# Two attention and MLP blocks on one core: the instruction order from the framework's timeline-simulating scheduler

## The chip, the cores and the metric

The kernel runs on one core of a Trainium2 chip. The metric is the device time of one execution in microseconds (us), the median of several runs. A core has five engines that run side by side: PE multiplies matrices (its weight loads are shown as PEld), DVE and ACT work elementwise, POOL does small set-up work, and SP here only issues DMAs. Each engine works off its own list of instructions strictly in the order of the list; semaphores make it wait for the others.

## The reference

Two models of depth 2 are run one after the other on one sequence of 256 tokens, width 1,024, in float32: first a block of attention layers (no MLP), then a block of attention and MLP layers.

```python
def first_block(x, ...):          # DEPTH = 2
    x = even_layer(x, ...)        # differential attention (4 heads) + forgetting attention (8)
    x = odd_layer(x, ...)         # sliding window with sinks (8) + chunked, relative bias (8)
def second_block(x, ...):         # DEPTH = 2
    x = x + dsa_mixer(rms_norm_2(x, g0), ...)          # index scores, top 64 keys, 16 heads
    x = x + squared_relu_mlp(rms_norm_2(x, m0), ...)   # 1024 -> 4096 -> 1024
    x = x + mla_mixer(rms_norm_2(x, g1), ...)          # latent q and kv, 16 heads
    x = x + squared_relu_mlp(rms_norm_2(x, m1), ...)
    return rms_norm_2(x, final_norm)
```

Every layer is: norm, projection in, attention per head (scores, bias or mask, softmax, weighted sum), projection out, residual. An MLP is `relu(h @ w_up)` squared, times `w_down`.

## The kernel before

**Work.** The state x lies transposed in SBUF (`xT`, 128 partitions x 8 x 256). Every product runs in a three-part form on rounded operands: each float32 operand is split into a rounded high part and a low rest, and PE adds high x high, low x high and high x low. So each weight block of 128 x 1,024 is fetched by a DMA on SP (`fetch`, L127, tile `raw`, 4 buffers), copied to its high part by ACT (`wh`, L176, 4 buffers), and its rest is taken by DVE (`wl`, L177, 4 buffers), in pieces of 256 or 512 columns (`PIECE`). PE then multiplies in `tokens` (L200), `tokens_apart` (L217) or `features` (L231); the sums stand in PSUM banks: `mm` 3, `s` 2, `tp` 2, `pv` 1 (`PS_BUFS`).

**Stages.** `forward` sets the layer number N.layer to 0 to 5: even layer, odd layer, sparse attention, MLP, latent attention, MLP. The stages lie at about 0 to 180, 180 to 300, 300 to 400, 400 to 580, 580 to 662 and 662 to 866 us; the projection out of one stage overlaps the next. In an attention stage a head's softmax goes: scores on PE (L506 or L518, bank `s`), adding the bias and taking the minimum of the negated scores on DVE (L534, `sx`, `mx`), exponential on ACT (L537, `se`), division (L545, L547), three transposes on PE (L553 to L555, bank `tp`), a split by ACT and DVE (L556, L557, `pt`), and the weighted sum on PE (L572, L587, L589, L606, L610, bank `pv`). Norms end in a reciprocal root, which `rsqrt` works out in nine short steps on DVE (L110 to L120); the head norm then scales `u` (L447), which PE transposes (L399).

**What sets the order.** Nothing in the code fixes the order on an engine. The functions are traced in one sequence; inside an attention stage that is a string of unit names (`ORDER0` to `ORDER3`), for example AW = weights of a head of the differential attention, BT = transposes of a forgetting head, GG = a gate. Every traced instruction gets a priority, its place in the trace; `N.ahead` moves it forward or back by an offset of the table `AHEAD` (weight splits under the key W). [...]

[...]

The change touches the function `kernel`, at the line that opens the `TileContext` (L1506).

## Time and profile before

| | |
|---|---|
| median of 3 runs | 866.77 us (865.86, 866.77, 868.64) |
| the profiled execution's own time | 868.05 us |
| its span, first to last instruction | 866.4 us |
| instructions | 17,641, of them 6,554 matmuls and as many weight loads |
| busy: PE, PEld, DVE, ACT, POOL | 97%, 93%, 77%, 67%, 5% of the span |
| DMA | 138.09 MB, 159 GB/s on average |
| granted TensorE clock, mean | 0.996 of full speed |

The profile is one execution with every instruction's start and length. A group names the line, the engine, the operation and its tiles (`out<-in`); a matmul's end is modelled and includes the time in the pipeline, so the records of neighbouring matmuls overlap. "Idle before" is the time in which the engine stood still ahead of these instructions, with the work that released it. [...]

### The profile page before, as it was taken

The numbers are of one execution on the slowest core, as the hardware profiler recorded it, in microseconds if no ns is written. First come the engines' busy times: TensorE is split into PE (matmuls) and PEld (weight loads), VectorE is DVE, ScalarE is ACT, GpSimd is POOL, SyncE is SP. The second block draws the span as 40 slices with busy tenths as digits, with TensorE's granted clock in tenths as the row PEclk, the third lists the DMA queues.
The fourth block names the chain that finished last, engine by engine and source line by source line (L and its number), as shares of the span: only waits on it lengthen the run. The fifth ranks groups of instructions, "written<-read, shape, count | busy, mean of one in ns | idle before, by whom it ended". The sixth has DMA issues, their size and how long they took to land. (4 is left out here: it accounts for less than half of the span.)

```text
span 866.4 us, 17641 instructions
## 1 busy us (share of the span) xinstructions
PE 840.8 (97%) x6554; PEld 808.7 (93%) x6554; DVE 670.6 (77%) x1799; ACT 577.7 (67%) x1379; POOL 40.7 (5%) x90
## 2 busy tenths in 40 slices
PE   6899999999999999999999999998999999999996
PEld 6899999999999999899999999998999998899986
DVE  6779997889898789988665576678999865557654
ACT  6597985779796576976654455556997665346542
POOL 9100000001000100000000000002000000000000
PEclk9999999999999999999999999999999999999999
DMA  7544344644634632246656656543324565555651
GB/s 263 166 161 139 107 142 158 198 158 143 230 97 160 184 108 91 97 137 184 191 194 190 180 192 194 187 139 104 112 73 157 183 190 180 186 187 184 218 163 48
DMA packets 40677, 138.09 MB, mean 159 GB/s; under 512 B 4960, under 2 KB 7152, under 8 KB 40592
## 3 DMA queue, kind: packets, MB, share of 16 engines
q1 hardware_dynamic: 39456, 134.20, 47.9%
q0 software_dynamic: 848, 2.25, 0.9%
q8 instruction: 51, 0.84, 0.4%
q10 hardware_dynamic: 288, 0.52, 0.2%
q14 instruction: 34, 0.28, 0.1%
HBM read 135.91 MB, written 1.05 MB: 158 GB/s over the span
## 5 line engine op out<-in xcount | busy, mean ns | idle before, releaser
L176 ACT ACTIVATE wh<-raw 128x512 fp32r<-128x512 f32 (+2 forms) x548 | 289.8, 570 | 202.8 <-issue 103.2
L177 DVE TENSOR_TENSOR wl<-raw,wh 128x512 fp32r<-128x512 f32 (+2 forms) x548 | 322.4, 618 | 115.6 <-ACT wh L176 111.9
L231 PE MATMUL mm<-ar,wh 128*128 128x256 f32 (+1 forms) x1664 | 301.0, 281 | 0.5 <-ACT ar L714 0.5
L231 PEld LDWEIGHTS mm<-ar,wh 128*128 128x128 f32 (+1 forms) x1664 | 255.0, 188 | 2.0 <-ACT ar L714 1.3
L200 PE MATMUL mm<-wh,ar 128*128 128x256 f32 (+2 forms) x1168 | 237.4, 299 | 8.1 <-ACT wh L176 6.6
L231 PE MATMUL mm<-ar,wl 128*128 128x256 f32 x832 | 232.8, 281 | 0.0
L200 PEld LDWEIGHTS mm<-wh,ar 128*128 128x128 f32 x1168 | 187.9, 192 | 13.4 <-ACT wh L176 6.7
L200 PE MATMUL mm<-wl,ar 128*128 128x256 f32 (+2 forms) x584 | 173.9, 298 | 1.1 <-DVE wl L177 1.1
L231 PEld LDWEIGHTS mm<-ar,wl 128*128 128x128 f32 x832 | 155.9, 188 | 0.3 <-DVE wl L177 0.2
L200 PEld LDWEIGHTS mm<-wl,ar 128*128 128x128 f32 x584 | 111.7, 191 | 4.3 <-DVE wl L177 1.9
L231 PE MATMUL s<-ar,wh 128*128 128x256 f32 x512 | 90.4, 279 | 0.0
L231 PEld LDWEIGHTS s<-ar,wh 128*128 128x128 f32 x512 | 77.9, 188 | 0.0
L231 PE MATMUL s<-ar,wl 128*128 128x256 f32 x256 | 71.4, 279 | 0.0
L537 ACT ACTIVATE se<-sx,mx 128x256 f32<-128x256 f32 (+1 forms) x128 | 57.2, 452 | 4.8 <-DVE mx L534 4.3
L231 PEld LDWEIGHTS s<-ar,wl 128*128 128x128 f32 x256 | 48.1, 188 | 0.0
L231 PE MATMUL pv<-ar,wh 128*128 128x256 f32 x256 | 45.1, 279 | 0.0
L231 PEld LDWEIGHTS pv<-ar,wh 128*128 128x128 f32 x256 | 39.0, 188 | 0.0
L231 PE MATMUL pv<-ar,wl 128*128 128x256 f32 x128 | 35.7, 279 | 0.0
L557 DVE TENSOR_TENSOR pt<-tp,pt 128x384 fp32r<-128x384 f32 x60 | 32.2, 552 | 3.5 <-ACT pt L556 2.8
L506 PE MATMUL s<-kbh,ar 128*128 128x512 f32 (+1 forms) x112 | 31.2, 355 | 0.5 <-ACT kbh L410 0.4
L556 ACT ACTIVATE pt<-tp 128x384 fp32r<-128x384 f32 x60 | 27.9, 486 | 1.1 <-PE tp L555 0.7
L1217 ACT ACTIVATE ar<-u 128x512 fp32r<-128x512 f32 x32 | 20.3, 633 | 11.7 <-DVE u L1215 11.7
(307 smaller groups left out, 1145.8 us busy)
## 6 DMA issues: line engine op xcount, KB each, us to landing
raw<-in_weights SPq DMA_DIRECT2D x242, 512.0 KB, 3.6
bias<-in_alibi SPq DMA_DIRECT2D x12, 192.0 KB, 2.8
bias<-in_relpos POOLq DMA_DIRECT2D x8, 192.0 KB, 2.8
raw<-in_weights SPq DMA_DIRECT2D x4, 384.0 KB, 2.8
xT<-in_x SPq DMA_DIRECT2D x4, 256.0 KB, 4.8
raw<-in_weights SPq DMA_DIRECT2D x4, 192.0 KB, 2.3
raw<-in_weights SPq DMA_DIRECT2D x2, 256.0 KB, 4.4
ar<-in_final_norm POOLq DMA_DIRECT2D x2, 256.0 KB, 5.2
```

The lines of the kernel that those rows point to most:

```text
L176: nc.scalar.activation(hi[:, c:e], raw[:, c:e], AF.Copy)
L177: nc.vector.tensor_tensor(out=lo[:, c:e], in0=raw[:, c:e], in1=hi[:, c:e].bitcast(F32), op=OP.subtract)
L200: nc.tensor.matmul(view[t], lhsT=x[:, s], rhs=w[:, j, :], start=(k + j == 0 and i == 0 and (t == 0 or not one)), stop=(k + j == nkt - 1 an ...
L231: nc.tensor.matmul(acc[:width, m * T:(m + 1) * T], lhsT=w[:, j, m * P:m * P + width], rhs=x, start=(k + j == 0 and i == 0 and m == 0), sto ...
L506: nc.tensor.matmul(o, lhsT=a_[:, gq, qt * P:(qt + 1) * P], rhs=b_[:, gk, 0:n], start=(i == 0), stop=(i == 2 and last))
L537: nc.scalar.activation(e[:, c:c + n], x[:, c:c + n], AF.Exp, bias=m[:, i:i + 1], scale=-1.0, accum_out=z[:, i:i + 1])
L556: nc.scalar.activation(h, p[:, :W], AF.Copy)
L557: nc.vector.tensor_tensor(out=l, in0=p[:, :W], in1=h.bitcast(F32), op=OP.subtract)
L1217: nc.scalar.activation(h, u, AF.Copy)
```

## The change

The `TileContext` is told to schedule on the timeline simulator instead of the default one. Nothing else is different.

```diff
@@ -1503,7 +1503,7 @@
     aps["weights"] = nc.dram_tensor("in_weights", (1, size), F32, kind="ExternalInput").ap()
     out = nc.dram_tensor("out_0", (1, T, D), F32, kind="ExternalOutput").ap()
     plan = []
-    with tile.TileContext(nc) as tc:
+    with tile.TileContext(nc, schedule_with_timeline_sim=True) as tc:
         forward(tc, aps, out, plan)
     assert sum(nk * P * nco for _, _, _, _, nk, _, nco in plan) == size
     arrays["in_weights"] = packed(inputs, plan, size)
```

## Rows read from the trace of the kernel before

**Rows 1.** The page, part 1: busy time (share of the span) and instructions

```profile
PE 840.8 (97%) x6554; PEld 808.7 (93%) x6554; DVE 670.6 (77%) x1799; ACT 577.7 (67%) x1379; POOL 40.7 (5%) x90
```

**Rows 2.** Busy time by stage; columns as in the first line

```profile
core 0: us, PE busy (x) PEld busy (x) DVE busy (x) ACT busy (x) POOL busy (x), PEclk, DMA share, GB/s
0.00:48.00 48.00, 36.46 (x257) 35.14 (x258) 35.42 (x123) 30.04 (x67) 23.59 (x50) 0.96 0.61 208
48.00:400.00 352.00, 348.49 (x2773) 335.65 (x2772) 310.60 (x980) 278.30 (x750) 8.08 (x22) 1.00 0.44 146
400.00:580.00 180.00, 180.00 (x1546) 180.00 (x1545) 118.56 (x200) 96.44 (x172) 1.21 (x2) 1.00 0.59 186
580.00:662.00 82.00, 79.09 (x596) 74.95 (x595) 76.81 (x262) 66.81 (x197) 5.25 (x12) 1.00 0.29 96
662.00:866.40 204.40, 196.81 (x1394) 182.96 (x1392) 129.24 (x238) 106.12 (x195) 2.53 (x4) 0.99 0.55 173
```

**Rows 3.** The chain that ended last: start us, us, what

```profile
648.02 0.87 PE tp L1361 x8
...
688.48 5.60 PE mm L231 x48
```

**Rows 4.** Waits of PE, by what they waited for: total us, times, longest

```profile
PE mm L200 <- ACT wh L176: 6.6, 1, 6.6
PE tp L399 <- DVE u L447: 3.9, 2, 3.7
...
PE pv L587 <- ACT pt L556: 0.4, 2, 0.2
...
PE tp L553 <- ACT se L537: 0.3, 1, 0.3
```

**Rows 5.** Busy time around the first stall; columns as in rows 2

```profile
30.00:34.00 4.00, 0.57 (x4) 0.57 (x5) 4.00 (x21) 0.79 (x2) 0.00 (x0) 0.96 0.47 169
34.00:37.40 3.40, 3.40 (x19) 3.40 (x18) 3.40 (x6) 2.23 (x5) 0.00 (x0) 0.54 0.48 164
```

**Rows 6.** PE by shape, 28 to 38 us: count, busy, mean, idle before

```profile
L200 PE MATMUL mm<-wh,ar 128*128 128x256 f32 x13 | 3.6, 361 | 0.0
L200 PE MATMUL mm<-wl,ar 128*128 128x256 f32 x6 | 2.2, 372 | 0.0
L399 PE MATMUL tp<-ident,u 128*128 128x128 f32 x8 | 2.0, 397 | 3.7 <-DVE u L447 3.7
L148 PE MATMUL mm<-ar,wn 128*128 128x256 f32 x14 | 1.8, 279 | 0.0
```

**Rows 7.** Timeline in the stall: start, us, engine, line, what, idle before

```profile
29.13 0.17 DVE L110 TENSOR_SCALAR rs_a<-ms 128x16 int32<-128x16 int32 x1
...
30.64 0.28 DVE L1060 TENSOR_SCALAR nturn<-ang 128x48 f32<-128x48 f32 x2
...
32.09 0.69 DVE L177 TENSOR_TENSOR wl<-raw,wh 128x512 fp32r<-128x512 f32 x1
32.69 1.28 DVE L447 TENSOR_TENSOR u<-u,rs_y 128x512 f32<-128x512 f32 x2
...
33.43 0.92 PE L399 MATMUL tp<-ident,u 128*128 128x128 f32 x4 [3.71 <-DVE u L447]
```

**Rows 8.** Groups of the page: count, busy us, mean ns, idle before

```profile
L557 DVE TENSOR_TENSOR pt<-tp,pt 128x384 fp32r<-128x384 f32 x60 | 32.2, 552 | 3.5 <-ACT pt L556 2.8
```

**Rows 9.** DVE by shape from 48 to 400 us; columns as in rows 6

```profile
L177 DVE TENSOR_TENSOR wl<-raw,wh 128x512 fp32r<-128x512 f32 x115 | 75.7, 683 | 4.0 <-ACT wh L176 3.4 <-PE mm L200 0.3
```

**Rows 10.** Line L110, first step of each reciprocal root: count, ns, start

```profile
L110 DVE TENSOR_SCALAR rs_a<-ms x8: 164/167/174, 29.1 to 215.3; 128x16 int32<-128x16 int32 x6, 128x12 int32<-128x12 int32 x1, 128x8 int32<-128x8 int32 x1
L110 DVE TENSOR_SCALAR rs_a<-st_v x6: 160/160/164, 25.3 to 683.1; 128x2 int32<-128x2 int32 x6
...
L110 DVE TENSOR_SCALAR rs_a<-lv x2: 169/264/358, 584.1 to 598.3; 128x2 int32<-128x2 int32 x2
```

**Rows 11.** Waits of SP's queue; columns as in rows 4

```profile
SPq L127 <- DVE wl L177: 570.7, 210, 10.2
```

## The prediction

> **What bounds the kernel now.** I read the page's busy shares first, then the same by stage, then PE's own waits, then the one place where PE stands still in mid-program.
>
> PE is busy for 840.8 of 866.4 us and DVE for 670.6 [rows 1]. By stage the kernel is of two kinds [rows 2]. From 400 to 580 us, the first MLP, PE has no idle time, and DVE and ACT are busy for 118.56 and 96.44 us of 180: only matrix products count, and the order on the other engines has 61 us of slack on DVE. From 662 us to the end, the last projection and the second MLP, it is the same but for the tail. The attention stages are tight: from 48 to 400 us DVE is busy for 310.60 of 352 us beside PE's 348.49, and from 580 to 662 us for 76.81 of 82. There two engines have to be fed at once, and the order of instructions decides whether they are.
>
> What can PE lose or win? Its gaps are 11.54 us before 48 us (48.00 less 36.46), 3.51 from 48 to 400, 2.91 from 580 to 662, and 7.59 from 662 on, nearly all behind the last matmul [rows 2]. Since matmul records overlap, a slow pace can hide in a busy PE. The weight loads show it: they are busy for 180.00 of 180 us in the first MLP, but for 335.65 of 352 and 74.95 of 82 in the two attention stages [rows 2]. So at most 16.35 + 7.05 = 23.4 us are to be won there, against the 6.42 us that PE's own idle time would allow. [...]
>
> PE's waits [rows 4] say where order matters. 6.6 us are the wait for the first weights. Then 3.9 us for u of L447, nearly all in one wait of 3.7 us. For the softmax tiles (tp from se, pv from pt) PE waits 0.3 and 0.4 us in all: of 60 tiles [rows 8], nearly every one comes in time.
>
> That wait of 3.7 us is the only example in this trace of a chain that the order breaks up, so I price it. From 29.13 us DVE works off the reciprocal root of the first head norm; between its short steps stand trigonometry for the fourth stage (nturn) and weight splits of 0.69 us, and PE gets its u only at 33.43 us [rows 7]. [...] PE's work from 28 to 38 us is 13 + 6 + 14 = 33 matmuls of 256 columns and 8 transposes [rows 6]. At full pace 48 such matmuls take 5.60 us, 116.7 ns each, and 8 transposes 0.87 us [rows 3]: 3.85 + 0.87 = 4.72 us. The stretch took 10, so one broken chain costs 5.3 us: 3.7 of idle time, 1.6 of slow clock.
>
> **The change, part by part.** It adds and removes no operation, no byte and no buffer. What may change is which ready instruction an engine gets next, and with it the order on PE, DVE, ACT, POOL and SP and the buffer each tile falls into. The priorities (trace order less the offsets in AHEAD) stay; what changes is the clock by which the scheduler thinks an instruction becomes ready. Where that clock differs, an instruction of lower priority is taken because the better one seems not ready, and on the chip the better one then stands behind it.
>
> Both MLP stages: 0. Sequence there is fixed by weight blocks, and DVE's 61 us and ACT's 84 us of free time per 180 [rows 2] hide a swap. Without that cover, each swap would cost one split of 0.683 us [rows 9].
>
> Softmax tiles: each of the 60 passes DVE and ACT before PE can go on. If one weight split of 0.683 us [rows 9] is put ahead of a step of each, the ends are 0 (always hidden) and 60 x 0.683 = 41.0 us (all of it reaches PE). Today's rows lie near the lower end: 0.7 us of PE waits on these tiles [rows 4], and DVE has 352 - 310.60 = 41.4 us free from 48 to 400 [rows 2] in which to catch up. I take a quarter, 10.2 us; the share is an estimate.
>
> Root chains: lines L110 to L120 run 8 times for head norms, 6 times for layer norms and twice for latents ahead of PE work [rows 10]. One of these 16 stalls PE today. The ends are -5.3 us (that one is cured) and 15 x 5.3 = 79.5 (all others stall too). The rows are nearest to the lower end, since 15 go by nearly free; another order has no reason to know which one PE waits for, so I take two more stalls: 2 x 5.3 = 10.6 us. Counting the idle time alone it would be 2 x 3.7 = 7.4.
>
> Queues: SP issues the weight loads in order and waits 570.7 us in 210 waits, the longest 10.2 us, until DVE has read a buffer [rows 11]. A bias load moved behind such a wait comes up to 10.2 us late; moved ahead, it holds a weight load up by one issue. POOL is busy for 40.7 us [rows 1], but its queue also issues DMAs, among them the eight relative biases. I take 0 for both, with -2 to +10.2 us as bounds: the loads stand several blocks ahead now, and a single late one is the price. The head up to the first matmul and the tail keep their dependencies: 0, and a few us either way, inside the bounds of the chains.
>
> Sum: 10.2 + 10.6 = 20.8 us. The profiled execution took 868.05 us (span 866.40 and 1.65 around it), 1.28 above the median of 866.77. So 868.05 + 20.8 = 888.85 in the terms of that execution, and 887.6 against the median.
>
> **Rivals.** First, faster: the other clock is nearer to the chip's, and steps on the way to PE come earlier. Place: the stages from 48 to 400 and 580 to 662 us, where up to 23.4 us of weight-load time lie free. For it: these us exist, and the stall at 30 us shows that today's order is not the best. Against: DVE is busy for 88% and 94% of these stages, and no order shortens its work. If half is won, 11.7 us, the time is 866.77 - 11.7 = 855.1. It decides from the point where it wins more than the broken chains cost, two of which eat 10.6 of it.
>
> Second, no change: the priorities alone fix the order, or the two clocks agree wherever it matters, and engines swap only work that nobody waits for. For it: 0.7 us of waits on 60 tiles show margins. Against: 1,799 DVE and 1,379 ACT instructions [rows 1] give many places in which a near tie is settled otherwise. 866.8 us.
>
> Third, much slower: tiles are late throughout, since two score banks, two transpose banks and one output bank pass a delay on to the next tile instead of absorbing it. Then all 41.0 us reach PE, and two chains break: 868.05 + 41.0 + 10.6 - 1.28 = 918.4 us. Against: projections are ready for PE most of the time.
>
> **How the numbers follow.** A difference of 0.3%, 2.6 us, is about what a measurement of this kernel can tell from none. The forecast and its surroundings up to some 905 us have 0.54, much slower 0.15, no change 0.09, faster 0.22. So slower by over 0.3% 0.69, same 0.09, faster 0.22. The predicted time is 887.6 us. The range runs from 855, half the room won, to 918, every tile late; about 0.08 lies below and 0.10 above. The slower cases alone would have 870 to 918.
>
> **What would show it.** Right: PE's idle time from 48 to 400 us grows from 3.51 by about 10 us, with waits on tp, pv or u from DVE and ACT; there are two or more gaps of about 3 us with a granted clock near the lower level behind them; 400 to 580 stays without idle time; the operations and their counts stay the same. Wrong: PE's weight loads from 48 to 400 rise above 335.65 us per 352, or the loss comes in the MLP stages, which I gave nothing, or from SP's queue.

## The result and the profile after

The changed kernel takes 910.3 us (median of 4 runs, 908.45 to 910.53) beside 867.7 us for the kernel before on the same chip: a ratio of 1.0496, 95% interval 1.0475 to 1.0517, or 42.6 us more. The forecast had slower, 887.6 us; the change is twice its size, inside the range and nearest to the third rival's 918.4.

The profiled execution took 910.38 us, its span 908.6 us. The same operations ran in the same numbers (page of the changed kernel, part 1, against [rows 1]):

```profile
PE 854.7 (94%) x6554; PEld 817.4 (90%) x6554; DVE 668.5 (74%) x1799; ACT 577.8 (64%) x1379; POOL 34.9 (4%) x90
```

Where the time went shows when both executions are cut at the same place of the work: the start of the fourth add to the residual (L301, on VectorE) that ends each stage. First the kernel before, then the changed one, busy time by stage (even, odd, sparse, first MLP, latent, the rest); columns as in [rows 2].

```profile
0.00:163.13 163.13, 151.10 (x1188) 146.97 (x1189) 135.67 (x423) 122.59 (x290) 25.10 (x56) 0.99 0.48 164
163.13:288.35 125.22, 124.29 (x996) 119.90 (x995) 110.58 (x357) 100.64 (x300) 6.10 (x15) 1.00 0.49 164
288.35:395.79 107.44, 105.35 (x811) 99.71 (x810) 95.60 (x314) 81.59 (x222) 0.47 (x2) 1.00 0.39 122
395.79:576.83 181.04, 181.04 (x1555) 181.04 (x1554) 119.60 (x202) 97.50 (x174) 1.21 (x2) 1.00 0.60 187
576.83:676.91 100.08, 97.17 (x749) 92.89 (x748) 93.66 (x293) 79.54 (x222) 5.25 (x12) 1.00 0.35 114
676.91:866.40 189.49, 181.90 (x1268) 168.19 (x1266) 115.52 (x213) 95.83 (x175) 2.53 (x4) 0.99 0.54 171
```

```profile
0.00:168.19 168.19, 154.56 (x1188) 150.14 (x1189) 135.26 (x423) 123.31 (x290) 20.34 (x56) 0.96 0.47 160
168.19:297.41 129.22, 125.69 (x1003) 120.61 (x1002) 110.16 (x357) 101.24 (x301) 6.56 (x16) 1.00 0.47 156
297.41:422.30 124.89, 107.83 (x810) 100.69 (x809) 98.15 (x315) 82.81 (x222) 0.00 (x0) 0.95 0.35 106
422.30:602.75 180.45, 180.45 (x1550) 180.45 (x1549) 117.93 (x202) 95.23 (x173) 1.21 (x2) 1.00 0.59 188
602.75:719.94 117.19, 104.92 (x752) 97.62 (x751) 93.23 (x293) 81.33 (x223) 4.26 (x12) 0.96 0.29 97
719.94:908.60 188.66, 181.23 (x1264) 167.91 (x1262) 113.80 (x213) 93.84 (x175) 2.52 (x4) 0.99 0.54 171
```

The length of a stage is the second number (the even stage's counts from the start of the span). The sparse stage lost 17.45 us and the latent stage 17.11; even and odd stage lost 5.06 and 4.00, and both MLP stages changed by less than 1 us. The busy times of DVE and ACT in a stage hardly moved: these engines have no more to do.

PE's busy time is 13.8 us longer (854.68 less 840.84, the sums over the stages) for the same 6,554 matmuls, most of it for the clock. Before, the granted clock stood at 0.50 of full speed, the lowest it shows, in one stretch in mid-kernel, 3.4 us at the stall of [rows 5]. Now it does in six, three in the even stage, one in the sparse and two in the latent stage, each around or behind idle time of PE; the three short ones, 3.4 us each, came behind waits of 1.3 to 1.7 us. They last 37.5 us in all, and PE is busy for 28.0 us of them. The longest of each stage, columns the same:

```profile
129.39:136.22 6.83, 6.08 (x27) 5.99 (x28) 6.51 (x13) 3.53 (x8) 0.32 (x2) 0.50 0.22 77
358.09:371.74 13.65, 6.26 (x19) 4.84 (x20) 11.75 (x65) 7.10 (x26) 0.00 (x0) 0.50 0.05 20
620.91:627.74 6.83, 5.39 (x23) 5.09 (x24) 4.86 (x17) 3.43 (x9) 1.12 (x4) 0.50 0.10 29
```

By the clock of 0.50 the same work at full clock would keep PE busy for about half of that, so the slow stretches cost PE some (28.0 - 3.4) / 2 = 12.3 us, an estimate. The other 28.4 us by which the span grew are idle time of PE (53.9 us, 25.6 before).

Inside the sparse stage the loss has one place. The changed kernel in slices, columns the same:

```profile
317.00:327.00 10.00, 10.00 (x88) 10.00 (x87) 7.79 (x27) 7.45 (x20) 0.00 (x0) 1.00 0.52 157
327.00:337.00 10.00, 10.00 (x82) 9.73 (x81) 8.38 (x19) 7.78 (x21) 0.00 (x0) 1.00 0.56 161
337.00:347.00 10.00, 10.00 (x81) 9.72 (x81) 9.84 (x26) 6.84 (x19) 0.00 (x0) 1.00 0.44 122
347.00:357.00 10.00, 6.59 (x53) 6.26 (x52) 9.76 (x30) 5.14 (x13) 0.00 (x0) 1.00 0.52 146
357.00:367.00 10.00, 1.77 (x4) 1.01 (x5) 9.26 (x47) 2.99 (x11) 0.00 (x0) 0.55 0.13 49
```

PE is full at first, then starved while DVE is full. What DVE does there is the top-k (L1144 and L1145, 16 rounds on one engine), and the heads' tiles cannot be used before its mask. In the kernel before, the same top-k ran beside projections: of its 20 us from 318 to 338, PE was busy for 19.70 (the first two rows; a third follows them).

```profile
318.00:328.00 10.00, 9.81 (x84) 9.65 (x83) 9.97 (x33) 5.53 (x11) 0.00 (x0) 1.00 0.38 113
328.00:338.00 10.00, 9.89 (x77) 9.35 (x77) 9.88 (x41) 7.20 (x17) 0.00 (x0) 1.00 0.12 46
338.00:348.00 10.00, 8.90 (x73) 8.56 (x72) 9.82 (x47) 7.85 (x26) 0.00 (x0) 1.00 0.50 154
```

So the top-k is late against the projections. The chain that leads to it (norm, index queries and key, transposes, four index scores, their sum) can be followed in the timelines: start, us, engine, line, what. Kernel before:

```profile
304.27 0.37 ACT L688 ACTIVATE gm<-mm 72x256 f32<-72x256 f32 x1
304.70 0.34 PE L695 MATMUL tp<-ident,gm 72*128 72x72 f32 x2
...
307.60 0.41 PE L399 MATMUL tp<-ident,gm 128*128 128x128 f32 x2
...
310.18 0.72 PE L506 MATMUL s<-kbh,ar 128*128 128x512 f32 x2
...
318.70 0.42 DVE L1144 MAX8 m<-bias 128x8 f32<-128x256 f32 x1
```

Changed kernel:

```profile
312.28 0.38 ACT L688 ACTIVATE gm<-mm 72x256 f32<-72x256 f32 x1
...
318.90 0.29 PE L695 MATMUL tp<-ident,gm 72*128 72x72 f32 x2
...
325.10 0.38 PE L399 MATMUL tp<-ident,gm 128*128 128x128 f32 x2
...
330.38 0.87 PE L506 MATMUL s<-kbh,ar 128*128 128x512 f32 x4
...
346.45 0.42 DVE L1144 MAX8 m<-bias 128x8 f32<-128x256 f32 x1
```

The index key is copied out 15.9 us after the start of the stage before, and 14.9 after: it is even earlier. But PE takes up its transposes 0.06 us after the copy's end before (304.27 + 0.37 to 304.70), and 6.24 us after it now (312.66 to 318.90). In those 6.24 us PE ran 47 projection matmuls and the 8 transposes of the two index queries, which stand ahead in its queue (PE by shape, 312.66 to 318.90 us):

```profile
L200 PE MATMUL mm<-wh,ar 128*128 128x256 f32 x32 | 6.0, 283 | 0.0
L200 PE MATMUL mm<-wl,ar 128*128 128x256 f32 x15 | 4.3, 286 | 0.0
L399 PE MATMUL tp<-ident,u 128*128 128x128 f32 x8 | 1.2, 273 | 0.0
```

The order of TensorE's queue held here: a transpose whose data had been there for 6.24 us did not pass a matmul.

Not all of the 6.24 us was lost to projections alone: the transposes of the queries took the two `tp` banks at 314.13 and 315.51 us, and DVE had read the first one out (L420) at 316.58. For the last 2.3 us the key had its data and a free bank, and only projections stood before it.

The chain falls further behind at every link, and not on PE's queue alone. The third index score, for example, ends on PE at 339.92 us, and ACT takes up its result only at 341.01, behind weight copies (L176) and others (L1098). In us after the start of the stage, from the two timelines:

| link of the chain | before | after | later by |
|---|---|---|---|
| sums of the norm, PE L338 | 5.5 | 7.7 | 2.2 |
| first query's transposes, PE L399 | 12.0 | 16.7 | 4.7 |
| key's first transposes, PE L695 | 16.4 | 21.5 | 5.1 |
| key's second transposes, PE L399 | 19.3 | 27.7 | 8.4 |
| first index score, PE L506 | 21.8 | 33.0 | 11.1 |
| fourth index score, PE L506 | 27.2 | 46.4 | 19.1 |
| top-k, DVE L1144 | 30.4 | 49.0 | 18.7 |
| end of the stage | 107.4 | 124.9 | 17.5 |

From the top-k to the end the stage takes 77.1 us before and 75.9 after. The whole loss lies ahead of the top-k.

PE's waits (columns as in [rows 4]) name where the projections had run out, not where the delay arose:

```profile
PE s L506 <- DVE mx L534: 11.9, 3, 7.9
PE mm L200 <- ACT wh L176: 7.1, 2, 6.9
PE mm L231 <- ACT ar L714: 5.9, 5, 1.7
PE mm L231 <- ACT ar L1273: 3.3, 1, 3.3
PE pv L606 <- ACT pt L556: 2.5, 5, 0.8
```

The 11.9 us are scores of the first heads: they wait for a score bank, which the softmax (L534) gives free only once the mask is there. And the tiles, which the forecast watched, wait longer too (before in [rows 8], now in this row): 9.2 us of DVE's idle time instead of 3.5.

```profile
L557 DVE TENSOR_TENSOR pt<-tp,pt 128x384 fp32r<-128x384 f32 x60 | 32.5, 551 | 9.2 <-ACT pt L556 9.1
```

### The profile page after: what moved, and what is told of

It is laid out like the page before. It is cut to its first block, busy times and chain, and to the rows that moved or that the text cites. A ratio compares the mean times of both kernels' runs of the same rounds, so it can differ in the third digit from the quotient of the medians.

```text
span 908.6 us, 17693 instructions
## 1 busy us (share of the span) xinstructions
PE 854.7 (94%) x6554; PEld 817.4 (90%) x6554; DVE 668.5 (74%) x1799; ACT 577.8 (64%) x1379; POOL 34.9 (4%) x90
## 4 chain that ended last, share of the span: by engine, by line
PE 85%; DVE 8%; ACT 5%; issue 1%; DMA 1%; SPq 0%; DVEq 0%; ACTq 0%
PE mm L231 31%; PE mm L200 24%; PE s L231 10%; PE pv L231 5%; PE s L506 3%; PE s L200 2%; DVE wl L177 2%; PE pv L200 1%; ACT se L537 1%; PE tp L399 1%; PE pv L587 1%; DVE sx L534 1%; ACT pt L556 1%; ACT wh L176 1%; PE mm L217 1%
## 5 line engine op out<-in xcount | busy, mean ns | idle before, releaser
L176 ACT ACTIVATE wh<-raw 128x512 fp32r<-128x512 f32 (+2 forms) x548 | 285.4, 569 | 237.5 <-issue 112.7
L177 DVE TENSOR_TENSOR wl<-raw,wh 128x512 fp32r<-128x512 f32 (+2 forms) x548 | 321.4, 619 | 141.3 <-ACT wh L176 140.3
L231 PE MATMUL mm<-ar,wh 128*128 128x256 f32 (+1 forms) x1664 | 309.8, 285 | 11.0 <-ACT ar L714 5.9
L231 PEld LDWEIGHTS mm<-ar,wh 128*128 128x128 f32 (+1 forms) x1664 | 261.4, 192 | 15.1 <-ACT ar L714 7.2
L200 PE MATMUL mm<-wh,ar 128*128 128x256 f32 (+2 forms) x1168 | 233.7, 297 | 8.6 <-ACT wh L176 7.1
L231 PEld LDWEIGHTS mm<-ar,wl 128*128 128x128 f32 x832 | 159.5, 192 | 0.5
L537 ACT ACTIVATE se<-sx,mx 128x128 f32<-128x128 f32 (+1 forms) x128 | 56.8, 447 | 9.0 <-DVE mx L534 6.3
L506 PE MATMUL s<-kbh,ar 128*128 128x512 f32 (+1 forms) x112 | 31.4, 366 | 11.9 <-DVE mx L534 11.9
L556 ACT ACTIVATE pt<-tp 128x384 fp32r<-128x384 f32 x60 | 28.4, 483 | 11.1 <-PE tp L555 10.7
L506 PEld LDWEIGHTS s<-kbh,ar 128*128 128x128 f32 x112 | 19.5, 200 | 14.6 <-issue 12.5
```

The lines of the kernel that those rows point to most:

```text
L176: nc.scalar.activation(hi[:, c:e], raw[:, c:e], AF.Copy)
L177: nc.vector.tensor_tensor(out=lo[:, c:e], in0=raw[:, c:e], in1=hi[:, c:e].bitcast(F32), op=OP.subtract)
L200: nc.tensor.matmul(view[t], lhsT=x[:, s], rhs=w[:, j, :], start=(k + j == 0 and i == 0 and (t == 0 or not one)), stop=(k + j == nkt - 1 an ...
L231: nc.tensor.matmul(acc[:width, m * T:(m + 1) * T], lhsT=w[:, j, m * P:m * P + width], rhs=x, start=(k + j == 0 and i == 0 and m == 0), sto ...
L506: nc.tensor.matmul(o, lhsT=a_[:, gq, qt * P:(qt + 1) * P], rhs=b_[:, gk, 0:n], start=(i == 0), stop=(i == 2 and last))
L537: nc.scalar.activation(e[:, c:c + n], x[:, c:c + n], AF.Exp, bias=m[:, i:i + 1], scale=-1.0, accum_out=z[:, i:i + 1])
```

## The experiments

Theory 1: the new scheduler lets ready projections ahead of the links of an attention chain; the chain gets late, and at its end nothing is left to run beside it. Theory 2: softmax tiles are late behind weight splits on VectorE and ScalarE, the forecast's term in a larger size. Theory 3: the order of the DMA queues. In all runs an "edge" is an order of issue within one engine's queue, without a wait for the earlier instruction to finish.

Stage lengths of all runs, in us, by the same cut:

| run | even | odd | sparse | MLP | latent | median |
|---|---|---|---|---|---|---|
| before | 163.1 | 125.2 | 107.4 | 181.0 | 100.1 | 867.7 |
| changed | 168.2 | 129.2 | 124.9 | 180.5 | 117.2 | 910.3 |
| p1, p2, p3 | 170.3, 176.1, 176.9 | 137.4, 132.3, 131.6 | 125.1, 124.6, 124.1 | 181.1, 181.0, 180.5 | 113.9, 120.9, 116.3 | 920.5, 926.5, 920.6 |
| e1, hold in sparse | 166.1 | 129.3 | 124.4 | 180.6 | 117.1 | 908.9 |
| e2, priority | 166.8 | 129.2 | 127.6 | 180.5 | 115.6 | 912.7 |
| q1, three stages as before | 165.9 | 129.2 | 106.7 | 181.1 | 100.0 | 874.4 |
| d1, 18 links late | 162.2 | 125.3 | 122.3 | 180.2 | 102.2 | 884.9 |
| d2, latent links late | 163.3 | 125.1 | 107.7 | 181.1 | 118.3 | 886.8 |
| d3, sparse splits ahead | 163.1 | 125.0 | 129.9 | 181.0 | 100.4 | 890.8 |
| d4, even and odd links late | 174.8 | 132.6 | 107.7 | 181.0 | 100.1 | 884.5 |
| h1, head | 162.8 | 125.4 | 107.5 | 181.0 | 100.1 | 868.9 |
| k1, key first | 161.0 | 125.0 | 108.6 | 180.3 | 100.1 | 867.6 |

**One engine's order from the one scheduler, the rest made by the other (p1, p2, p3).** After the tracing of the program, an edge from each instruction of an engine (in p3 of two engines) to the next, in the order (`names`) that the other kernel has:

```diff
         forward(tc, aps, out, plan)
+        pinned(tc)
...
+        for one, two_ in zip(names, names[1:]):
+            tc.add_manual_dep(traced[two_], one, mybir.DependencyInfo(mybir.DependencyClass.NoSync,
+                                                                      mybir.DependencyReason.DATA), reason="pinned")
```

> The timeline scheduler as in the changed kernel, but TensorE's queue is held to the order of the kernel before (an issue-order edge from each matmul or transpose to the next, no wait); the other engines' orders stay the new scheduler's. Theory 1 (the loss is TensorE's order: ready projections are let ahead of the links of the attention chains, so the projections are used up before a stage's last softmax tiles): nearly all of the 43 us comes back, 858 to 872 us; the sparse stage 105 to 111 us (changed kernel 124.9), the latent stage 98 to 104 us (117.2). If the stall at 28 to 38 us that the change removed was VectorE's and ScalarE's order, it stays away and the time is below that of before, about 861. Theory 2 (the loss is the orders of VectorE and ScalarE: softmax tiles are late behind weight splits): 895 to 912 us, both stages still above 115 us. Theory 3 (the DMA queues' order): 900 to 912 us.

> The counterpart: the scheduler of the kernel before, with TensorE's queue held to the order of the changed kernel. Theory 1: the loss is made without the new scheduler's other orders, 895 to 915 us, sparse stage 120 to 127 us, latent stage 112 to 119 us. Theory 2: 866 to 880 us. Theory 3: 866 to 875 us.

> The timeline scheduler with VectorE's and ScalarE's queues held to the order of the kernel before, TensorE's left to the new scheduler. Theory 1: the projections still go ahead of the chains, 885 to 912 us. Theory 2: the loss is gone, below 878 us.

Measured: p1 920.5 us (1.0613, 1.0586 to 1.0641), p2 926.5 (1.0686, 1.0655 to 1.0717), p3 920.6 (1.0619, 1.0589 to 1.0649). p2 came out as Theory 1 has it, and beyond: the changed kernel's order on TensorE makes the loss without the new scheduler's other orders. But p1 contradicts Theory 1 as it was put: TensorE's old order under the new scheduler gives nothing back. Nor does p3, against Theory 2. These are no clean exchanges, since the scheduler makes the other queues anew around the forced one. In p1 and p3 the top-k starts 35.0 and 38.5 us after the start of the stage, neither the 30.4 of the one kernel nor the 49.0 of the other, and the stage is as long as in the changed kernel because 90.1 and 85.6 us follow instead of 75.9. All three runs are slower than either whole set of queues. So the loss does not go away with one engine's order; that each set of queues has to agree fits this, but no run shows why these mixtures are worse.

**Hold projections behind the index scores (e1).** In the changed kernel, four projections of `ORDER2` (queries SQ1, SQ2, SQ3 and values SV) may be issued on TensorE only behind the last index score (IS3):

```diff
...
-            with N.ahead(f):
+            behind = HOLD[N.layer].get(name)
+            with N.ahead(f), (tc.issue_after(ends[behind]) if behind else nullcontext()):
                 U[f](*args)
+            ends[name] = N.last
```

> The changed kernel with one hold in the sparse stage: four projections (SQ1, SQ2, SV, SQ3) may not be issued on TensorE before the last matmul of the index scores (IS3). By the order of the queues the last index score then stands 132 TensorE rows earlier than in the changed kernel (46 us of its 181 rows of delay against the kernel before are left to a queue of ready work). Theory 1: the top-k starts 8 to 15 us earlier in its stage and runs beside the held projections; the sparse stage falls from 124.9 to 108 to 118 us, the whole to 893 to 904 us, and the latent stage stays at 117 us. Theory 2: the tiles after the top-k are as late as they were, stage 122 to 127 us, whole 907 to 914 us.

(In that text "46 us" is a slip for 49 rows, 181 less 132.) Measured 908.9 us (1.0485, 1.0450 to 1.0519), stage 124.4: nearly nothing. The top-k did start earlier, 41.0 us into the stage instead of 49.0, but from there to the end it took 83.4 us instead of 75.9. In the slices of this run PE's idle time has moved ahead of the top-k, where the chain is still slow for its links on DVE and ACT, and there is a second gap behind it.

```profile
315.00:325.00 10.00, 6.82 (x59) 6.61 (x58) 7.70 (x27) 7.34 (x20) 0.00 (x0) 1.00 0.51 157
325.00:335.00 10.00, 7.96 (x39) 6.85 (x40) 7.84 (x18) 6.22 (x19) 0.00 (x0) 0.83 0.19 51
335.00:345.00 10.00, 10.00 (x84) 9.87 (x83) 9.51 (x32) 4.41 (x11) 0.00 (x0) 1.00 0.31 79
345.00:355.00 10.00, 10.00 (x87) 10.00 (x87) 9.77 (x34) 5.72 (x13) 0.00 (x0) 1.00 0.44 142
355.00:365.00 10.00, 5.47 (x41) 5.09 (x39) 9.34 (x40) 6.36 (x21) 0.00 (x0) 0.87 0.67 204
```

Why the earlier start won nothing shows on DVE: with the held projections their weight splits came to stand between the 16 rounds of the top-k. The splits alone, from the first round to the last, in this run (its L180 is L177 of the others) and in the changed kernel:

```profile
core 0: us, DVE busy (x), PEclk, DMA share, GB/s
336.36:362.36 26.00, 10.83 (x16) 1.00 0.48 143
346.45:365.65 19.20, 4.10 (x6) 0.80 0.35 107
```

The rounds took 26.0 us instead of 19.2 (20.9 before, with 8 splits), and the whole mask, which the heads wait for, was ready 68.2 us after the start of the stage, against 68.7 in the changed kernel and 52.5 before. From there to the end it is 56.2, 56.1 and 55.0 us. So it is the end of the top-k, not its start, that goes with the end of the stage: in e2, d1 and d3 below the mask comes at 71.6, 68.3 and 72.0 us, and 54 to 58 us follow. Only in p1 and p3 (62.5 and 61.1 us) does more follow, 63 us.

**Make the loss in the kernel before (d1).** Theory 1 in its second form says where the loss arises, ahead of the top-k, so it has to be possible to make it there and nowhere else. The old scheduler, and 18 edges: each of nine links of the index chain and nine of the latent stage's first chain behind the projection matmul that stands last before it in the changed kernel.

```diff
         forward(tc, aps, out, plan)
+        held(tc)
...
+    for late, early in BEHIND:
+        tc.add_manual_dep(traced[f"I-{late}"], f"I-{early}", mybir.DependencyInfo(
+            mybir.DependencyClass.NoSync, mybir.DependencyReason.DATA), reason="held")
```

> The kernel before, with its own scheduler, and 18 issue-order edges on TensorE alone: each of nine links of the index chain in the sparse stage (sums, transposes, four index scores) and nine of the latent stage's first chain may be issued only behind the projection matmul that stands last before it in the changed kernel. Theory 1, in its form after the last runs (a chain link that waits behind ready projections starts the next link late on every engine; top-k then starts some 18 us later, and what follows top-k takes 76 us as before): sparse stage 120 to 126 us (107.4 before), latent stage 108 to 118 us (100.1), whole 888 to 906 us; the top-k starts 44 to 50 us after its stage (30.4 before). Rival 4 (the loss needs VectorE's and ScalarE's orders too, TensorE's placement of the links alone is absorbed): both stages within 4 us of before, whole 866 to 876 us.

Measured 884.9 us (1.0208, 1.0191 to 1.0226). In the sparse stage it is as Theory 1 said: top-k 50.1 us after the start, stage 122.3, that is 14.9 of the changed kernel's 17.5 us. The slices have the changed kernel's shape, full, then starved at a slow clock:

```profile
328.00:338.00 10.00, 10.00 (x77) 9.46 (x76) 9.61 (x24) 6.61 (x19) 0.00 (x0) 1.00 0.50 155
338.00:348.00 10.00, 7.00 (x60) 6.79 (x58) 9.86 (x33) 6.02 (x14) 0.00 (x0) 1.00 0.47 142
348.00:358.00 10.00, 2.77 (x7) 1.75 (x8) 9.48 (x54) 3.44 (x14) 0.00 (x0) 0.51 0.23 66
```

In the latent stage the expectation failed: 102.2 us, 2.1 lost of 17.1. Nine links of its first chain do not make the loss there.

**All links of the latent stage (d2).** The same with 248 edges for every transpose, score and value matmul of that stage.

> The kernel before with its own scheduler and issue-order edges on TensorE in the latent stage alone: every transpose, score and value matmul of the stage that stands behind a projection matmul in the changed kernel, and ahead of it in the kernel before, is held behind it (248 edges; the run with nine links gave 102.2 us). Theory 1: the loss of this stage lies in the links of all its waves of heads, 110 to 121 us (changed kernel 117.2, whole order of TensorE under the old scheduler 120.9); whole 877 to 888 us. Rival 6 (in the latent stage the placement against projections costs nothing, the other engines' orders do it): under 104 us, whole 865 to 871 us.

Measured 886.8 us (1.0228, 1.0195 to 1.0261), the latent stage 118.3 us. The old scheduler, with TensorE's links placed as in the changed kernel, makes the loss of that stage in full; it is spread over three waves of heads, whose last softmax begins at 80.5 us before and 95.2 in the changed kernel, from the stage's start.

**The splits instead of the projections (d3).** In the sparse stage, edges on DVE (215) and ACT (108) alone: behind a weight split what stands behind it in the changed kernel.

> The kernel before with its own scheduler and issue-order edges on VectorE (215) and ScalarE (108) in the sparse stage alone: what stands behind a weight split there in the changed kernel, and ahead of it in the kernel before, is held behind it; TensorE is left to the old scheduler. Theory 1 in its wide form (an engine's queue with ready work, or work that waits for a weight buffer, ahead of a link makes the chain late, whichever engine it is): the top-k starts 40 to 50 us after its stage, the stage takes 117 to 125 us, the whole 876 to 886 us. Rival 7 (TensorE alone, the splits fit between the links): stage under 112 us, whole under 872 us.

Measured 890.8 us (1.0280, 1.0253 to 1.0306), the stage 129.9 us, above the expected 125; top-k 53.2 us after the start. So splits ahead of the links do it as well, and more. A loss that TensorE's order can make alone, and VectorE's and ScalarE's alone too, need not go when only one of them is put right. That fits e1, where splits between the rounds took the time that was won. In p1 too 14 splits stand there (9.4 us), and the mask comes 10.0 us later than in the kernel before; the other 7.7 us of its loss in this stage lie behind the mask and stay unexplained.

**Even and odd stage (d4).** TensorE's links there, 360 edges.

> The kernel before with its own scheduler and issue-order edges on TensorE in the even and the odd stage alone (360 edges): what stands behind a projection matmul in the changed kernel, and ahead of it in the kernel before, is held behind it. The head's stall of 3.7 us goes with it, since its transposes now stand behind the third projection block. Theory 1: the two stages lose what they lost in the changed kernel or a little more (whole order of TensorE under the old scheduler: 176.1 and 132.3 us): even stage 166 to 176 us (163.1 before, 168.2 changed), odd stage 128 to 133 us (125.2 and 129.2), the whole 873 to 888 us. Rival 8 (in these two stages the loss of 9 us is from the DMA or VectorE's order and not the placement on TensorE): both within 2 us of before, 865 to 870 us.

Measured 884.5 us (1.0193, 1.0169 to 1.0216): 174.8 and 132.6 us, 11.7 and 7.4 lost. The placement costs in these stages too. It costs more than the 5.1 and 4.0 of the changed kernel, as in p2, where the old scheduler makes the other queues too. d1 to d4 all make their losses with no edge on a DMA queue, so Theory 3 is not needed for them; an exchange of the DMA queues' order alone was not run.

**Give three stages back whole (q1).** The new scheduler, every engine's queue as before from the sparse to the end of the latent stage.

> The timeline scheduler, with every engine's queue held to the order of the kernel before from the sparse stage to the end of the latent stage; even and odd stage, head and tail stay the new scheduler's. Theory 1: those stages come back whole (125 to 107.4 and 117.2 to 100.1 us), 910.3 - 17.5 - 17.1 = 875.7, so 871 to 880 us; the even and odd stage keep their 5.1 and 4.0 us. Rival 5 (the crossed runs were slow because any forced order costs time by itself, or the semaphores differ): 885 to 912 us.

Measured 874.4 us (1.0089, 1.0073 to 1.0106), expected 875.7; stages 106.7 and 100.0 us. It also shows that held queues cost nothing by themselves. What is left, 7.1 us against the 867.3 us of this comparison, is about the 2.8 and 4.0 us of the even and the odd stage.

**Priority (e2).** The index chain of the changed kernel at priority 4000 ahead of its place (the scores by `'IS': 4000` in `AHEAD`, the rest as here):

```diff
+    urgent = ExitStack()
+    urgent.enter_context(tc.high_priority(offset=4000))
     index_q(0)
...
+    urgent.close()
```

> The changed kernel with the index chain's priority raised above everything (offset 4000 for the index projections, splits, key and scores). Theory 1: the new scheduler does not hold an engine for a link that is about to become ready and lets ready work of any priority ahead of it, so the links lie as late: the first index score stands at TensorE's row 2501 (2453 in the changed kernel), 908 to 916 us. Rival (the offsets, tuned for the other scheduler, are what is wrong): the top-k starts 10 us earlier, 890 to 902 us.

Measured 912.7 us (1.0525, 1.0506 to 1.0544); the top-k starts 54.9 us after the start of the stage. Offsets tuned for the other scheduler are not the reason here: more urgency does not get the links ahead.

**Cure the head's stall in the kernel before (h1).** The old scheduler and a single edge: the transposes that kept PE idle for 3.7 us [rows 7] go behind the 40th matmul of the third projection block.

> The kernel before with one issue-order edge: the first transposes of the head norm (tp, at 33.4 us, for which TensorE stood idle 3.7 us) are issued behind the 40th matmul of the third projection block, as the new scheduler does. Theory 1b (the stall at 28 to 38 us was a link put in the queue ahead of ready projections, before its data): the stall of 3.7 us and the slow clock behind it go, 860 to 864 us. Rival: the projections are missing later in the even stage, 865 to 870 us.

Measured 868.9 us against 867.3 (1.0015, 1.0002 to 1.0028). The stall went, and with it the slow clock behind it; the time did not. It is no clean cure: a smaller stall of 1.9 us came in its place, before 39.44 us (L692 on PE, for `ar` of DVE, L423). PE's instructions from 20 to 40 us and from 40 to 60, first the kernel before, then this run:

```profile
20.00:40.00 20.00, 16.29 (x124) 16.05 (x123) 14.88 (x63) 9.46 (x20) 5.03 (x16) 0.91 0.61 195
40.00:60.00 20.00, 18.73 (x153) 18.29 (x153) 14.85 (x59) 18.19 (x46) 0.00 (x0) 1.00 0.37 127
```

```profile
20.00:40.00 20.00, 18.06 (x155) 17.86 (x154) 16.97 (x75) 11.69 (x23) 4.57 (x14) 1.00 0.67 204
40.00:60.00 20.00, 17.57 (x136) 16.55 (x136) 15.37 (x51) 18.72 (x47) 0.00 (x0) 1.00 0.39 122
```

31 matmuls more in the first stretch, 17 fewer in the second: most of the projections used to fill the gap are missing in the next stretch. The even stage takes 162.8 us instead of 163.1.

**The key ahead of the second query (k1).** In the kernel before, the index key is traced ahead of the second index query.

> The kernel before with its own scheduler; in the sparse stage the index key and its split are traced ahead of the second index query, so that the first index score comes some 40 TensorE rows (4.7 us) earlier and the last one 11 rows (1.3 us). If the start of top-k sets the end of the stage also downwards: top-k starts 1 to 3 us earlier, stage 104.5 to 106.5 us (107.4), whole 864 to 866.5 us. Rival (what follows top-k is bound by VectorE's total work): stage 107 to 108 us, whole 866 to 868 us.

Measured 867.6 us against 866.6 (1.0014, 0.9998 to 1.0030). The top-k started 30.1 us after the start of the stage, only 0.3 earlier than before, so this says nothing on a top-k that is earlier. No version here beats the kernel before.

## Why the prediction was right in sign and half in size

The mechanism stands in the forecast's part on the change: an instruction is taken because a better one seems not ready, and the better one then stands behind it. The second half is in the trace, up to 6.24 us for a link of the index chain; the first, what seems ready to the scheduler, is the author's reading and shown by no run. Slower was right, and so was nothing for both MLP stages (181.04 to 180.45 us, and 189.49 to 188.66 for the last). The queues' 0 holds as far as PE shows it: its only long wait for weights is still the first one, 6.9 us now and 6.6 before [rows 4]. SP's longest wait for a buffer did grow past its bound, from 10.2 to 36.2 us (356 to 392 us), without a wait of PE for those weights.

The step that failed is the term of the softmax tiles, 10.2 us. It was the sum's only term for a link that stands behind other work, it counted no links but those of tiles, and it took its price from one weight split, 0.683 us, and a quarter of 60 tiles. Measured, a link of the index chain stood up to 6.24 us behind other work, mostly projections, nine times that price; the links before the top-k, which are not tiles at all and had no term, lost 18.7 us together, and one serial chain adds them up. In d1, nine such links make 14.9 us. In the latent stage the links of all waves of heads make the loss (d2, 18.2 us), and there too it begins ahead of the tiles: the first softmax starts 42.7 us after the start of the stage, 34.7 before. How much of the rest is the tiles' own is not shown. (The 0.7 us of waits that the term started from left out 0.3 us at L606; that is too little to matter.)

The cover named for that term was DVE's 41.4 us of free time from 48 to 400 us. It was free, and not where it was needed: during the top-k DVE is full (9.76 and 9.26 of 10 us), and of its idle time in the changed sparse stage 9.0 us lie ahead of the top-k and 17.1 behind it.

The term of the root chains, 10.6 us, half of the sum, had the wrong sign where it was taken from. The one stall in the trace went: in the changed kernel PE is busy for all of 20 to 40 us, and no wait for `u` of L447 is longer than 0.34 us. Nor is its price of 5.3 us to be had back: in h1, where it shrank to one of 1.9 us without a slow clock, the time did not fall. A gap in which projections do not run need be no loss while they are a reserve that a later gap uses. The slow-clock gaps that the forecast wanted as a sign came, six of them at a granted clock of 0.50, yet not from root chains; with two stalls it had 2 x 1.6 = 3.2 us for the clock, against the 12.3 estimated above. Its 1.6 us are a remainder, 10 - 4.72 - 3.7, of a stretch with 3.4 us at 0.54 [rows 5].

The forecast's own sign shows the size: PE's idle time was to grow by about 10 us from 48 to 400; to 422, the same point of the work within a few us, it grew from 3.5 to 27.1 (374 less PE's 346.90 us). The rival of 918.4 us came nearest in size, by lateness of all 60 tiles, which is not how it came about; that it came so near is luck, as is that the measured time lies inside the range.

Open: why the new scheduler places the links so late. The runs show where they stand and that priority does not move them (e2), not how the scheduler comes to it. How the loss of the even and odd stages divides between the queues was not tried beyond d4, and why one engine's old order beside new queues is slower than either kernel is not known.

## What to carry to other kernels

Ready bulk work is a reserve for the stretches in which a serial chain holds the other engines. An order that puts it ahead of the chain's links spends that reserve early, and each link then pays the queue ahead of it: up to 6.24 us here, and 18.7 us for the whole chain to the top-k. So price a change of order from the longest serial chain of each stage, links times the work that may stand ahead of one, not from idle time. Follow the chain to its last link: an earlier start, here by 8.0 us, is worth next to nothing when the work that it frees then stands between the later links (e1, 908.9 us against 910.3). And an engine's gap that later work refills can be worth nothing (h1, 868.9 us against 867.3): look for the stretch in which bulk work runs out.

## What was not expected of the hardware

The gap of TensorE at the top-k cost a second time, in the chain links behind it: around the 7.9 us of idle time before 361.48 us the granted clock was 0.50 (358.09 to 371.74 us; mean 0.55 in the slice from 357 to 367 us and 0.76 in the next one), when the heads' links came. The transposes of one tile then took 0.41 to 0.42 us each; those of a tile at 372.27 us, back at a clock of 1.00, took 0.27.

```profile
361.48 1.19 PE L506 MATMUL s<-kbh,ar 128*128 128x512 f32 x2 [7.88 <-DVE mx L534]
...
369.50 0.41 PE L553 MATMUL tp<-ident,se 128*128 128x128 f32 x1
```
